# A bilinear form on one core: the first float32 weight group in two transfers, two rows of each partition and then the other six

## The chip, the cores and the metric

The kernel runs on one core of one Trainium2 chip. The metric is the device time of one execution in microseconds, as the median of several runs; smaller is better. The profile's own span, from the first to the last instruction, is a little shorter than that time.

## What is computed

```python
batch, dim_i, dim_j, dim_k = 32, 256, 256, 128
# x: [32, 256], y: [32, 256], weight: [128, 256, 256], all float32
out = np.einsum('bi,bj,kij->bk', x, y, weight)   # [32, 128]
```

The weight is 128 x 256 x 256 x 4 bytes = 33.6 MB and is read once. x, y and the result are small beside it (32, 32 and 16 KB).

## The kernel before

The 128 values of k are laid out as 4 blocks of 32 "groups". A group g is one slice of the weight in SBUF of 128 partitions x 8 rows of 256 values (IC = 8 rows, J = 256), 1 MB in float32, or 8 KB in each partition. For each group TensorE multiplies the 8 rows, one after the other, by a 128 x 128 matrix built from x, and adds them up in PSUM; VectorE multiplies the sum by y and reduces it to one column of the result.

The matmuls take bfloat16. Thirty of the 32 groups come by GpSimd's queue, whose transfers turn float32 into bfloat16 on the way. Two groups, 0 and 16, come as float32 by the queues of SyncE and ScalarE and are then cast by ScalarE. All transfers are placed at the head of the program, ahead of everything else on their engines.

```python
LOADS = (                       # GpSimd's transfers: groups, first row, last row
    ((8, 24), 0, 8),
    ((4, 12, 20, 28), 0, 8),
    (tuple(range(2, 32, 4)), 0, 8),
    (tuple(range(1, 32, 4)), 0, 8),
    ((3, 11, 19, 27), 0, 8),
    ((7, 23), 0, 8),
    ((15,), 0, 8),
    ((31,), 0, 4), ((31,), 4, 6), ((31,), 6, 7), ((31,), 7, 8),
)
FIRST = (0, 16)                 # the two float32 groups
# ... cut ...
    w_sb = sbuf("w_sb", [P, G, IC * J], bf16)
    w_f = sbuf("w_f", [P, len(FIRST), IC * J], f32)
# ... cut ...
    hw = [
        nc.scalar.dma_start(out=x_sb, in_=x).then_inc(s_x, 16).ins,
    ]
    for n, (g, queue) in enumerate(zip(FIRST, (nc.sync, nc.scalar))):
        hw.append(
            queue.dma_start(
                out=w_f[:, n:n + 1, :], in_=rows_of((g,)),
            ).then_inc(s_f[n], 16).ins
        )
# ... cut: hw and GpSimd's transfers are moved to the head of the program ...
    for n, g in enumerate(FIRST):           # ScalarE casts the float32 groups
        for h in range(2):
            lo, hi = h * IC * J // 2, (h + 1) * IC * J // 2
            c = act.copy(out=w_sb[:, place_of[g], lo:hi], in_=w_f[:, n, lo:hi])
            if h == 0:
                c._wait_ge(s_f[n], 16)
            c.then_inc(s_act, 1)
# ... cut: VectorE builds the matrix from x, and y4 from y ...
    pe.wait_ge(s_act, 2 * len(FIRST))
    pe.wait_ge(s_dve, t_x)
    # for each unit of 16, 8, 4, 2, 1 and 1 groups: matmuls over 8 rows, each waiting for
    # its groups' transfer, then VectorE's multiplication by y4 and reduction
# ... cut ...
    sp.dma_start(out=out_v, in_=acc)._wait_ge(s_dve, n_dve).then_inc(s_out, 16)
```

The six units of TensorE are of 16, 8, 4, 2, 1 and 1 groups. The first holds groups 0 and 16 and all that GpSimd's first three weight transfers bring; the last is group 31, which comes in four small pieces.

Of the kernel before, what the change touches and what calls it, by code (L numbers as in the profile page):

```python
# [29 lines left out]
)  # L30

FIRST = (0, 16)
BANKS = 8


@with_exitstack
def kernel(
# [7 lines left out]
    nc = tc.nc  # L45
# [8 lines left out]
    _, J = y.shape  # L54
# [11 lines left out]
    def sbuf(name, shape, dtype):  # L66
        return nc.alloc_sbuf_tensor(name, shape, dtype).ap()

    def rows_of(groups):


        step = G // len(groups)
        assert all(g == groups[0] + n * step for n, g in enumerate(groups))
        v = weight.rearrange("(u s) (ip ic) j -> s ip u (ic j)", s=step, ic=IC)
        return v[groups[0]]

    def w_of(groups):
        at = [place_of[g] for g in groups]
        step = at[1] - at[0] if len(at) > 1 else 1
        assert all(a == at[0] + n * step for n, a in enumerate(at))  # L80
        return w_sb[:, at[0]:at[-1] + 1:step, :]

    w_sb = sbuf("w_sb", [P, G, IC * J], bf16)
    w_f = sbuf("w_f", [P, len(FIRST), IC * J], f32)
    x_sb = sbuf("x_sb", [B, I], f32)
# [10 lines left out]
    acc = sbuf("acc", [P, G], f32)  # L96
    ps = nc.alloc_psum_tensor("ps", [P, BANKS, 2, J], f32).ap()

# [4 lines left out]
        for s, (groups, lo, hi) in zip(s_w, LOADS) for g in groups for ic in range(lo, hi)  # L103
    }
    s_f = [nc.alloc_semaphore(f"f{g}") for g in FIRST]
    s_x = nc.alloc_semaphore("x")
# [14 lines left out]
            out=w_of(groups)[:, :, lo * J:hi * J],  # L121
            in_=rows_of(groups)[:, :, lo * J:hi * J],
# [6 lines left out]
    hw = [  # L129
        nc.scalar.dma_start(out=x_sb, in_=x).then_inc(s_x, 16).ins,  # L130
    ]
    for n, (g, queue) in enumerate(zip(FIRST, (nc.sync, nc.scalar))):
        hw.append(
            queue.dma_start(
                out=w_f[:, n:n + 1, :], in_=rows_of((g,)),
            ).then_inc(s_f[n], 16).ins
        )
    for ins in [*hw, *sw]:
        tc.no_tile_sem_insts.add(ins.name)

# [8 lines left out]
    for blk in blocks:  # L149
# [20 lines left out]
        out=ident, in_=ident, compare_op=mybir.AluOpType.not_equal, fill=1.0,  # L170
# [3 lines left out]

    for n, g in enumerate(FIRST):
        for h in range(2):
            lo, hi = h * IC * J // 2, (h + 1) * IC * J // 2
            c = act.copy(out=w_sb[:, place_of[g], lo:hi], in_=w_f[:, n, lo:hi])  # L178
            if h == 0:
                c._wait_ge(s_f[n], 16)  # L180
            c.then_inc(s_act, 1)


# [2 lines left out]
    def done(ins):  # L186
# [6 lines left out]
        out=x_rep,  # L193
        in_=x_sb.rearrange("b (ip ic) -> b ic ip", ic=IC).unsqueeze(3)
        .to_broadcast([B, IC, IP, KK]),
    )._wait_ge(s_x, 16))
    for q in range(Q):
        c = v.transpose(  # L198
            out=xt[q * 32:(q + 1) * 32, :, :],
            in_=x_rep[:, :, q * IP // Q:(q + 1) * IP // Q, :],  # L200
        )
# [4 lines left out]
        out=mask, in_=ident.rearrange("p (ip kk) -> p kk ip", kk=KK), axis=AX, op=add,  # L206
    )._wait_ge(s_pool, 2))

    for kk in range(KK):
        c = v.tensor_scalar(  # L210
            out=xblk[:, :, :, kk], in0=xt, scalar1=mask[:, kk:kk + 1],
            scalar2=None, op0=mult,
        )
# [6 lines left out]
        out=yt, in_=y_sb.rearrange("b (jb j) -> b jb j", j=32),  # L220
    )._wait_ge(s_y, 16))
    t = done(v.tensor_copy(  # L222
        out=y_rep, in_=yt.unsqueeze(3).to_broadcast([B, J // 32, B, KK]),
    )._wait_ge(s_dve, t))
    BQ = B // Q
    for q in range(Q):
        c = v.transpose(  # L227
            out=y4[q * 32:(q + 1) * 32, :].rearrange("p (jb j) -> p jb j", j=32),
            in_=y_rep[:, :, q * BQ:(q + 1) * BQ, :],
        )  # L230
# [5 lines left out]
    def product(out, lhsT, rhs, first, last, load):  # L236
        return pe.add_instruction(mybir.InstMatmult(  # L237
            name=nc.get_next_instruction_name(), engine=mybir.EngineType.PE,
            ins=[pe.lower_ap(rhs), pe.lower_ap(lhsT)], outs=[pe.lower_ap(out)],
            start_tensor_calc=first, stop_tensor_calc=last,  # L240
            tile_size=(P, P), tile_position=(0, 0), ldweights=load,
        ))

    pe.wait_ge(s_act, 2 * len(FIRST))
    pe.wait_ge(s_dve, t_x)
    at_dve = t_x
    n_pe = 0
    freed = [0] * BANKS
    landed = set()
    p0 = bank = 0  # L250
    held = None
    for u, unit in enumerate(UNITS):

        n_g = len(unit)
        n_b = (n_g + 1) // 2
        if bank + n_b > BANKS:
            bank = 0
# [8 lines left out]
        for n_step, (ic, h) in enumerate(steps):  # L266
            n = n_g // n_b
# [7 lines left out]
            for s in need[:-1]:  # L275
                pe.wait_ge(s, 16)
            c = product(
                ps[:, bank + h, :n, :],
                xblk[:, ic, :, :].rearrange("p b kk -> p (b kk)"),
                w_sb[:, p0 + o:p0 + o + n, ic * J:(ic + 1) * J],  # L280
                first=(ic == order[0]), last=(ic == order[-1]), load=(held != ic),
            )
# [10 lines left out]
        if n_g > 1:  # L293
            t = done(v.tensor_tensor(  # L294
                out=prod, in0=sums, in1=y4.unsqueeze(1).to_broadcast([P, n_g, J]), op=mult,
# [3 lines left out]
                out=acc[:, unit[0]:unit[-1] + 1:unit[1] - unit[0]], in_=prod, axis=AX, op=add,  # L299
            )._wait_ge(s_dve, t))  # L300
        else:
            done(v.tensor_tensor_reduce(  # L302
                out=prod[:, 0, :], in0=sums[:, 0, :], in1=y4, scale=1.0, scalar=0.0,
# [44 lines left out]
```

## Time and profile before

| | before |
|---|---|
| time, median of 3 runs | 84.98 us (84.90 to 85.03) |
| span of the profiled execution | 83.4 us |
| TensorE matmul busy | 32.5 us (39%) |
| VectorE busy | 25.2 us (30%) |
| ScalarE busy | 5.2 us (6%) |
| GpSimd busy | 8.8 us (11%) |
| read from HBM | 33.62 MB |
| GpSimd's queue: packets, share of the 16 DMA engines | 4432, 94.4% |
| SyncE's queue | 288, 3.5% |
| ScalarE's queue | 192, 3.3% |
| float32 group from SyncE, issue to landing | 4.9 us |
| float32 group from ScalarE, issue to landing | 8.3 us |

Busy times are shares of the span; they overlap and don't add up to it. A transfer has two ends in the profile: the instruction with which an engine issues it, and its packets on the 16 DMA engines, which come later. Both are given in microseconds from the first instruction. The GB/s row counts the bytes written, so a transfer that turns float32 into bfloat16 shows half of what it reads. SyncE does nothing between its first transfer and the output.

### The profile page before, as it was taken

How to read it: one execution, taken by the hardware profiler on the slowest of the kernel's cores; microseconds unless marked ns; L12 is line 12 of the kernel's file. 1: busy time of each engine (PE TensorE's matmuls, PEld its weight loads, DVE VectorE, ACT ScalarE, POOL GpSimd, SP SyncE). 2: the span in 40 equal slices, each digit the busy share in tenths (PEclk: the TensorE clock that was granted, in tenths of full speed). 3: DMA queues.
4: the chain of work that ended last, by engine and by line, in shares of the span. 5: the costliest groups of instructions: out<-in, count | busy, mean ns of one | idle time of the engine just before them, and what ended most of it. 6: DMA issues, size and time to landing. Idle time of an engine off the chain costs nothing.

```text
span 83.4 us, 257 instructions
## 1 busy us (share of the span) xinstructions
PE 32.5 (39%) x136; PEld 4.3 (5%) x43; DVE 25.2 (30%) x28; ACT 5.2 (6%) x5; POOL 8.8 (11%) x18
## 2 busy tenths in 40 slices
PE   0000000000000000000099999996029999884780
PEld 0000000000000000000000000000000110112330
DVE  0009450000292000000000000003999800999932
ACT  0019930000000000000000000000000000000000
POOL 5999600000000000000000000000000000000000
PEclk9999999999999999999999999999995799999998
DMA  4999999999999999999999999999999999999980
GB/s 122 393 370 293 214 214 212 216 218 212 218 218 216 212 216 216 212 218 214 212 214 218 210 220 214 214 214 216 212 214 218 212 214 216 212 216 214 197 118 8
DMA packets 4912, 17.91 MB, mean 215 GB/s; under 512 B 384, under 2 KB 800, under 8 KB 4656
## 3 DMA queue, kind: packets, MB, share of 16 engines
q0 software_dynamic: 4432, 15.76, 94.4%
q1 hardware_dynamic: 288, 1.07, 3.5%
q10 hardware_dynamic: 192, 1.08, 3.3%
HBM read 33.62 MB, written 0.02 MB: 403 GB/s over the span
## 4 chain that ended last, share of the span: by engine, by line
DMA 46%; PE 39%; DVE 6%; POOL 3%; another core or an unknown queue 3%; issue 2%; POOLq 0%
DMA w_sb<-in_weight_dram 46%; PE ps L237 39%; DVE tmp L294 5%; POOL w_sb L120 2%; POOL y_sb L127 1%; DVE tmp L302 1%; POOL const-float32-0.0 L332 0%; POOLq L332 0%; POOL const-uint8-127 L332 0%; POOL const-float32-1.0 L332 0%; DVE acc L302 0%
## 5 line engine op out<-in xcount | busy, mean ns | idle before, releaser
L237 PE MATMUL ps<-w_sb,xblk 128*128 128x512 bf16 (+1 forms) x136 | 32.5, 396 | 48.9 <-DMA w_sb<-in_weight_dram 44.2
L294 DVE TENSOR_TENSOR tmp<-ps,y 128x4096 f32<-128x4096 f32 (+3 forms) x4 | 8.6, 2156 | 36.7 <-PE ps L237 36.6
L298 DVE TENSOR_REDUCE acc<-tmp 128x16 f32<-128x4096 f32 (+3 forms) x4 | 8.6, 2154 | 0.1
L237 PEld LDWEIGHTS ps<-w_sb,xblk 128*128 128x128 bf16 x43 | 4.3, 101 | 76.9 <-DMA w_sb<-in_weight_dram 42.7
L120 POOL DMA_DIRECT2D w_sb<-in_weight_dram x11 | 7.6, 707 | 0.6 <-issue 0.6
L178 ACT CAST w_sb<-w_f 128x1024 bf16<-128x1024 f32 x4 | 3.9, 1040 | 0.0
L219 DVE STREAM_TRANSPOSE yt<-y_sb 32x256 f32<-32x256 f32 x1 | 0.4, 433 | 10.9 <-DMA y_sb<-in_y_dram 10.9
L192 DVE COPY x_rep<-x_sb 32x1024 f32<-32x1024 f32 x1 | 0.8, 790 | 6.1 <-PEq L332 6.1
L227 DVE STREAM_TRANSPOSE y<-y_rep 32x256 f32<-32x256 f32 x4 | 1.7, 435 | 0.1
L198 DVE STREAM_TRANSPOSE xt<-x_rep 32x256 f32<-32x256 f32 x4 | 1.7, 435 | 0.1
L178 ACT ACT_TABLE_LOAD x1 | 1.3, 1283 | 6.0 <-PEq L332 6.0
L210 DVE TENSOR_SCALAR xblk<-xt,mask 128x256 bf16<-128x256 f32 x4 | 1.4, 499 | 0.0
L302 DVE CUSTOM_DVE_ANT_0 tmp<-ps,y 128x256 f32<-128x256 f32 x2 | 0.8, 424 | 1.6 <-PE ps L237 1.6
L222 DVE COPY y_rep<-yt 32x1024 f32<-32x1024 f32 x1 | 0.7, 682 | 0.0
L205 DVE TENSOR_REDUCE mask<-ident 128x4 f32<-128x128 f32 x1 | 0.4, 382 | 1.0 <-POOL ident L169 1.0
L127 POOL DMA_DIRECT2D y_sb<-in_y_dram x1 | 0.5, 534 | 0.0
L168 POOL MEMSET ident<- 128x128 f32 x1 | 0.3, 302 | 0.0
L169 POOL TENSOR_SCALAR_AFFINE_SELECT ident<-ident 128x128 f32<-128x128 f32 x1 | 0.3, 287 | 0.1
L302 DVE DVE_READ_ACCUMULATOR2_ANT acc<- 128x1 f32 x2 | 0.2, 84 | 0.0
L332 POOL MEMSET const-float32-0.0<- 128x1 f32 x1 | 0.1, 98 | 0.2 <-issue 0.2
L332 POOL MEMSET const-bfloat16-1.0<- 128x1 bf16 x1 | 0.1, 101 | 0.0
L332 POOL MEMSET const-uint8-127<- 128x1 uint8 x1 | 0.1, 101 | 0.0
(1 smaller groups left out, 0.1 us busy)
## 6 DMA issues: line engine op xcount, KB each, us to landing
w_sb<-in_weight_dram POOLq DMA_DIRECT2D x2, 4096.0 KB, 48.0
w_sb<-in_weight_dram POOLq DMA_DIRECT2D x2, 2048.0 KB, 43.3
w_sb<-in_weight_dram POOLq DMA_DIRECT2D x2, 1024.0 KB, 40.9
w_f<-in_weight_dram SPq DMA_DIRECT2D x1, 1024.0 KB, 4.9
w_f<-in_weight_dram ACTq DMA_DIRECT2D x1, 1024.0 KB, 8.3
w_sb<-in_weight_dram POOLq DMA_DIRECT2D x1, 512.0 KB, 72.1
w_sb<-in_weight_dram POOLq DMA_DIRECT2D x1, 256.0 KB, 72.7
w_sb<-in_weight_dram POOLq DMA_DIRECT2D x1, 128.0 KB, 72.9
```

Source lines behind the costliest of these rows:

```text
L120: nc.gpsimd.dma_start(out=w_of(groups)[:, :, lo * J:hi * J], in_=rows_of(groups)[:, :, lo * J:hi * J],).then_inc(s, 16).ins
L127: sw.insert(2, nc.gpsimd.dma_start(out=y_sb, in_=y).then_inc(s_y, 16).ins)
L178: c = act.copy(out=w_sb[:, place_of[g], lo:hi], in_=w_f[:, n, lo:hi])
L192: t = done(v.tensor_copy(out=x_rep, in_=x_sb.rearrange("b (ip ic) -> b ic ip", ic=IC).unsqueeze(3) .to_broadcast([B, IC, IP, KK]),)._wait_ ...
L198: c = v.transpose(out=xt[q * 32:(q + 1) * 32, :, :], in_=x_rep[:, :, q * IP // Q:(q + 1) * IP // Q, :],)
L210: c = v.tensor_scalar(out=xblk[:, :, :, kk], in0=xt, scalar1=mask[:, kk:kk + 1], scalar2=None, op0=mult,)
L222: t = done(v.tensor_copy(out=y_rep, in_=yt.unsqueeze(3).to_broadcast([B, J // 32, B, KK]),)._wait_ge(s_dve, t))
L227: c = v.transpose(out=y4[q * 32:(q + 1) * 32, :].rearrange("p (jb j) -> p jb j", j=32), in_=y_rep[:, :, q * BQ:(q + 1) * BQ, :],)
L237: return pe.add_instruction(mybir.InstMatmult(name=nc.get_next_instruction_name(), engine=mybir.EngineType.PE, ins=[pe.lower_ap(rhs), pe.l ...
L294: t = done(v.tensor_tensor(out=prod, in0=sums, in1=y4.unsqueeze(1).to_broadcast([P, n_g, J]), op=mult,)._wait_ge(s_pe, n_pe))
L298: done(v.tensor_reduce(out=acc[:, unit[0]:unit[-1] + 1:unit[1] - unit[0]], in_=prod, axis=AX, op=add,)._wait_ge(s_dve, t))
L302: done(v.tensor_tensor_reduce(out=prod[:, 0, :], in0=sums[:, 0, :], in1=y4, scale=1.0, scalar=0.0, op0=mult, op1=add, accum_out=acc[:, uni ...
```

## The change

SyncE's float32 group, one transfer of 8 rows (8 KB) of each partition, is cut into two on the same queue: rows 0 and 1 first, then rows 2 to 7. ScalarE's group stays whole. Both pieces count up the same semaphore, and the first cast of that group waits for 32 in place of 16. The purpose is to get the first bytes of the weight moving sooner: the first transfer that SyncE hands out is a small one.

```diff
 FIRST = (0, 16)
+
+FIRST_ROWS = (((0, 2), (2, 8)), ((0, 8),))
 BANKS = 8
@@
-    for n, (g, queue) in enumerate(zip(FIRST, (nc.sync, nc.scalar))):
-        hw.append(
-            queue.dma_start(
-                out=w_f[:, n:n + 1, :], in_=rows_of((g,)),
-            ).then_inc(s_f[n], 16).ins
-        )
+    for n, pieces in enumerate(FIRST_ROWS):
+        for lo, hi in pieces:
+            hw.append(
+                (nc.sync, nc.scalar)[n].dma_start(
+                    out=w_f[:, n:n + 1, lo * J:hi * J],
+                    in_=rows_of(FIRST[n:n + 1])[:, :, lo * J:hi * J],
+                ).then_inc(s_f[n], 16).ins
+            )
@@
-                c._wait_ge(s_f[n], 16)
+                c._wait_ge(s_f[n], 16 * len(FIRST_ROWS[n]))
```

Everything else, the instructions of TensorE, VectorE, ScalarE and GpSimd among it, is as before; SyncE has one issue more.

## The prediction

> **What bounds the kernel now.** I read the chain of waits first, then the waits, then the first microseconds cut into short stretches. In the chain of work that ended last, in order of time (start us, length us, what), these pieces carry the end:
>
> ```profile
> 3.18 38.65 DMA w_sb<-in_weight_dram
> ...
> 74.77 1.28 another core or an unknown queue
> ...
> 77.98 0.49 another core or an unknown queue
> ...
> 79.55 0.17 another core or an unknown queue
> ...
> 81.44 0.42 DVE tmp L302
> ```
>
> TensorE works in bursts and between them waits for something that is not an engine. The timeline names it: before the matmuls at 76.09, 78.51 and 79.76 us the releaser is the transfer of w_sb, with idle times of 1.32, 0.53 and 0.22 us. So the end hangs on the last bytes of the weight. The page's row of the 16 DMA engines' busy share over 40 slices of 2.1 us, and the rate below it, say whether that stream ever rests:
>
> ```profile
> DMA  4999999999999999999999999999999999999980
> GB/s 122 393 370 293 214 214 212 216 218 212 218 218 216 212 216 216 212 218 214 212 214 218 210 220 214 214 214 216 212 214 218 212 214 216 212 216 214 197 118 8
> ```
>
> It rests in the first slice and after the weight is in, nowhere else. The rate halves after the fourth slice because GpSimd's transfers read float32 and write bfloat16, and the row counts bytes written: 214 written are about 428 read. The end is therefore: when the stream gets going, plus the bytes over a fixed rate, plus a tail. The change touches only the first term and, a little, the second. The start, from the timeline (start us, length us of the issuing instruction):
>
> ```profile
> 0.00 0.63 SPq L134 DMA_DIRECT2D w_f<-in_weight_dram  x1
> 0.12 0.42 ACTq L130 DMA_DIRECT2D x_sb<-in_x_dram  x1
> ...
> 0.58 0.56 ACTq L134 DMA_DIRECT2D w_f<-in_weight_dram  x1
> 1.05 1.60 POOL L120 DMA_DIRECT2D w_sb<-in_weight_dram  x2 [0.61 <-issue]
> ```
>
> and the same time in stretches of 0.2 us; the last two columns are the DMA share and GB/s:
>
> ```profile
> 1.00:1.20 0.20, 0.00 (x0) 0.00 (x0) 0.00 (x0) 0.00 (x0) 0.15 (x1) 1.00 0.08 31
> 1.20:1.40 0.20, 0.00 (x0) 0.00 (x0) 0.00 (x0) 0.00 (x0) 0.20 (x1) 1.00 0.43 128
> 1.40:1.60 0.20, 0.00 (x0) 0.00 (x0) 0.00 (x0) 0.00 (x0) 0.20 (x1) 1.00 2.02 492
> 1.60:1.80 0.20, 0.00 (x0) 0.00 (x0) 0.00 (x0) 0.00 (x0) 0.20 (x1) 1.00 0.50 123
> 1.80:2.00 0.20, 0.00 (x0) 0.00 (x0) 0.00 (x0) 0.00 (x0) 0.20 (x2) 1.00 0.66 210
> 2.00:2.20 0.20, 0.00 (x0) 0.00 (x0) 0.00 (x0) 0.00 (x0) 0.20 (x1) 1.00 1.01 410
> ```
>
> A packet is counted where it starts, so single values jump. The sum from 1.0 to 2.0 us is (31 + 128 + 492 + 123 + 210) x 0.2 us = 197 KB; at the 410 GB/s that the next twelve stretches have on average (their sum is 4919), that is 0.48 us of work. The stream behaves as if it had begun at full rate at 2.00 - 0.48 = 1.52 us after the first instruction. That 1.52 us is all the change can win from. The packet records of the trace say what is in it: x, 32 packets of 1 KB, starts at 1.16 us, 1.04 us after its issue began; the first 8 KB packet of the SyncE transfer starts at 1.42 us, 1.42 us after its issue began. The first packets of this transfer take up to 594 ns, later ones mostly 309 to 345. ScalarE's float32 group starts only at 4.19 us, when SyncE's is nearly through, and GpSimd's first packet comes at 5.48 us.
>
> **What the Trainium skill says.** "DMA: Bandwidth & Descriptors", section "Latency and other measured facts", puts the first byte of a transfer from SyncE or ScalarE at about 0.6 us. The trace has 1.04 us (x) and 1.42 us (weight) from the beginning of the issuing instruction, and 0.63 and 0.79 us from its end; only the second count is near it. The same page, section "Issuing engines are not separate DMA queues", says that all issuers share the same 16 DMA engines and that more issues save only sequencer time. The trace agrees: once going, the rate is about 410 GB/s whoever issued. Its section "Rules for kernel authors" advises one large transfer rather than several small ones, which speaks against the change. Its section "Why a DMA increments its semaphore by 16 and not by 1" warns that of two transfers sharing a semaphore only the full count says that all has landed; the changed kernel does wait for 32, the full count, so no half-landed group is read.
>
> **The change part by part.** It removes one SyncE issue of 128 rows of 8 KB and puts two in its place: 128 rows of 2 KB, then 128 rows of 6 KB. Bytes, matmuls, casts and the other queues stay.
>
> Gained: an earlier first packet. The weight issue took 0.63 us and its first packet came 0.79 us later. The output transfer, also 128 rows from SyncE but of 128 B each, took 0.35 us to issue at 81.90 us and had its first packet at 82.74 us, 0.84 us after the issue began. So 128 rows need not cost 1.42 us; the longer rows, or being first, do. If the issue grows with the bytes of a row, a row of 2 KB lies a quarter of the way: 0.35 + (0.63 - 0.35)/4 = 0.42 us. First packet 0.63 to 0.79 us later, thus at 1.05 to 1.21 us instead of 1.42: a gain of 0.21 to 0.37 us, middle 0.29.
>
> Does a hole follow? The first piece is 8 packets of 2 KB per DMA engine. At 313 ns for 8 KB (the median in this queue) that is 8 x 78 = 0.63 us, plus some 0.28 us by which the first packet exceeds a later one (594 - 313): it lasts till about 1.13 + 0.63 + 0.28 = 2.04 us. The second issue can begin at 0.42 us and, taken like the whole one, has its first packet 1.42 us later, at 1.84 us, before the first piece ends. ScalarE's group is issued at 0.58 us as well. No hole is expected.
>
> Paid: packets. Each DMA engine has 8 more data packets and one more completion. The x packets of 1 KB took 44 ns where 313/8 = 39 would be in proportion, so 5 ns of overhead each; GpSimd's packets that write 1 KB from 2 KB took 98 ns where 324/4 = 81 is in proportion, 17 ns. So 9 more packets cost 9 x 5 = 0.05 to 9 x 17 = 0.15 us per engine, middle 0.10 us, and this lies on the path because the stream never rests.
>
> Beside the path: the extra issue on SyncE (some 0.5 us), which has nothing to do until 81.90 us; and w_f landing later. It landed 4.9 us after issue; should ScalarE's group now go in between, it might land at about 8.2 us. The four casts (1.04 us each, from 7.33 us) would then end about 1 us later, at 12.2 us, and TensorE doesn't start until 41.87 us.
>
> Sum: -0.29 + 0.10 = -0.19 us. I round it up a little in favour of the change, as the late first packets may shorten too, and take -0.23: 84.98 - 0.23 = 84.75 us.
>
> **The rivals.** First, the first packet doesn't come sooner: 1.42 us is set by being the first issue, or by x, whose packets run at 1.16 to 1.39 us on most engines just ahead. Against it stands that ScalarE's second issue, not its first, took 0.56 us for the long rows, and its first, with 32 short ones, 0.42. For it: the output transfer differs from the weight's in being late and alone as well as in row length, so the trace holds no clean pair; also one DMA engine had both its x packet and its first weight packet only at 1.93 us, which is no matter of row length. Then only the packets' cost remains: 84.98 + 0.10 = 85.08 us.
>
> Second, a hole between the pieces: the second issue waits behind x and ScalarE's issue, and its first packets pay the start again, up to 0.28 us (594 - 313). With the gain of 0.29 and the cost of 0.10 this makes 85.07 us. Against it: ScalarE's group would fill the hole, because it is queued from 1.14 us on.
>
> Third, a hidden gain: the stream ends earlier but TensorE doesn't follow. TensorE idles 1.32 us for the transfer at 76.09 us and 0.30 us at 71.16 us, so a stream earlier by 0.2 or 0.3 us pulls every later start. I give this little weight; it would leave 84.98 us.
>
> Fourth, a large loss, if 6 KB rows ran badly. The group is a 32nd of the weight, some 2.5 us of the stream. It would have to run at under 60% of its rate to cost 2%: 2.5/0.6 = 4.2 us. Nothing in the trace points there.
>
> **Range and chances.** The main line gives from -0.37 + 0.05 = -0.32 to -0.21 + 0.15 = -0.06 us, the rivals 0 to +0.15 us. I give the main line three chances in five. With the spread of the runs before (84.90 to 85.03) the range is 84.45 to 85.12 us. A change of 2% is 1.7 us, more than the whole 1.52 us before the stream starts, so faster by over 2% is practically shut out, and slower by over 2% needs the fourth rival: 0.01 faster, 0.98 within 2%, 0.01 slower.
>
> **What would show each step right or wrong.** Right: in the changed profile SyncE shows two issues, the first shorter than 0.63 us; short stretches show weight traffic before 1.4 us and no dip between 1.8 and 2.4 us; the effective start worked out as above falls from 1.52 to about 1.25 us; and the matmuls' waits for w_sb near the end, and the last w_sb packet at 80.79 us, come some 0.2 us earlier. The first issue as long as before, or a first packet at 1.4 us, proves the first rival; a dip after 2 us the second; an earlier last packet with the same end the third. The prediction is wrong if the time rises clearly although the first packet comes earlier: then the packets cost more than 17 ns each, or the order of the queues matters in a way that this profile doesn't show.

## Result and profile after

| | before | after |
|---|---|---|
| time, median | 84.91 us (84.69 to 85.03, 6 runs) | 87.21 us (87.06 to 102.13, 6 runs) |
| ratio after / before, 95% interval | | 1.0272 (1.0253 to 1.0292) |
| span of the profiled execution | 83.4 us | 85.9 us |
| last weight packet ends | 80.79 us | 83.28 us |
| SyncE's float32 group, first packet to last packet's end | 1.42 to 4.57 us | 1.40 to 4.99 us (2 KB rows), 5.43 to 12.20 us (6 KB rows) |

Ratios leave out executions over 1.5% above the fastest of their kernel: here the one of 102.13 us (granted clock 0.76), below two of flat_64_64 and one of pitch_10k.

The change costs 2.3 us. Two rows of the page show where: the busy share of the DMA engines and GB/s in 40 slices of 2.15 us, changed kernel.

```profile
DMA  2699999999999999999999999999999999999930
GB/s 61 189 354 320 293 226 214 216 216 218 216 214 216 218 214 218 214 218 214 214 214 214 214 216 214 214 214 214 214 216 214 216 214 214 218 210 213 193 47 8
```

The first two slices move 61 and 189 GB/s; before, they moved 122 and 393. From the seventh slice on the rate is that of before. So the loss is made in the first microseconds, up to about 5 us, and never given back. Cut finer, DMA share and GB/s in the last two columns, first the changed kernel:

```profile
1.40:2.00 0.60, 0.00 (x0) 0.00 (x0) 0.00 (x0) 0.00 (x0) 0.60 (x2) 1.00 0.42 126
2.00:3.00 1.00, 0.00 (x0) 0.00 (x0) 0.00 (x0) 0.00 (x0) 1.00 (x2) 1.00 0.37 96
3.00:4.00 1.00, 0.00 (x0) 0.00 (x0) 0.00 (x0) 0.00 (x0) 1.00 (x2) 1.00 0.90 254
4.00:5.00 1.00, 0.00 (x0) 0.00 (x0) 0.00 (x0) 0.00 (x0) 1.00 (x3) 1.00 0.85 281
5.00:6.00 1.00, 0.00 (x0) 0.00 (x0) 0.00 (x0) 0.00 (x0) 1.00 (x2) 1.00 1.03 424
```

and three of the same stretches before:

```profile
1.40:2.00 0.60, 0.00 (x0) 0.00 (x0) 0.00 (x0) 0.00 (x0) 0.60 (x2) 1.00 1.06 275
2.00:3.00 1.00, 0.00 (x0) 0.00 (x0) 0.00 (x0) 0.00 (x0) 1.00 (x2) 1.00 1.04 426
3.00:4.00 1.00, 0.00 (x0) 0.00 (x0) 0.00 (x0) 0.00 (x0) 1.00 (x2) 1.00 0.99 401
```

From 2 to 3 us, when all data packets are 2 KB rows, the changed kernel moves 96 GB/s where 426 were moved. The engines are then busy for 0.37 of the time, and 59% of the 2 KB packets took no more than 84 ns, about a quarter of the 309 ns of most 8 KB packets: much of the time is lost between the packets. The transfer's 16 completion packets of 4 bytes, which fit one for each DMA engine, show when each share of the 2 KB rows was done: eight at 2.72 to 3.31 us, the other eight at 3.87 to 4.99 us. ScalarE's group, from 3.12 us on, doesn't reach full rate before 5 us. Summed over the packet records, a packet's bytes spread evenly over its time, 1.75 MB had been read by 6.0 us before and 1.08 MB after; the missing 0.67 MB are 1.6 us at the 430 GB/s that were read from 10 to 75 us.

The profiled end came 2.5 us later; the remaining 0.9 us of that is unevenness. A transfer counts as complete with the last of 16 counts on its semaphore, one from each DMA engine: in the changed kernel the 16th count of the transfer that TensorE first waits for came at 44.32 us, and TensorE started at 44.37 us. The times of the first and the last of these 16 counts, from the trace's semaphore events:

```
transfer                         before              after
GpSimd's first weight transfer   11.97 to 12.45 us   13.14 to 14.95 us
GpSimd's last weight transfer    80.59 to 81.07 us   81.75 to 83.56 us
```

The earliest count is 1.2 us late, the latest 2.5 us, the mean of the 16 1.6 us, and all three stay so through 70 us. That fits engines that each keep a fixed share of every transfer; the records don't name the engines, so this is not shown. The end waits for the latest count. The chain that ended last shows the shift passing through (start us, length us, what; changed kernel):

```profile
3.17 41.15 DMA w_sb<-in_weight_dram
...
77.31 1.20 another core or an unknown queue
...
80.44 0.53 another core or an unknown queue
...
82.04 0.18 another core or an unknown queue
...
83.93 0.42 DVE tmp L306
```

The first wait for the weight grew by 2.50 us (from 38.65), the last VectorE step starts 2.49 us later (from 81.44), and the three waits in between that stand here are within 0.08 us of those before.

The timeline of the issues (changed kernel) answers the first question of the prediction:

```profile
0.00 1.27 SPq L137 DMA_DIRECT2D w_f<-in_weight_dram  x2
0.12 0.41 ACTq L132 DMA_DIRECT2D x_sb<-in_x_dram  x1
...
0.58 0.60 ACTq L137 DMA_DIRECT2D w_f<-in_weight_dram  x1
...
12.83 3.88 ACT L182 CAST w_sb<-w_f 128x1024 bf16<-128x1024 f32 x4 [5.51 <-DMA w_f<-in_weight_dram]
```

SyncE's two issues take 0.63 and 0.59 us (1.27 us with the pause between them); the small one is no shorter than the whole one was. The casts wait for the 6 KB rows and end at 16.7 us, far from TensorE's start at 44.37 us.

### The profile page after: what moved, and what is told of

The parts are those of the page before. It is cut to its first block, busy times and chain, and to the rows that moved or that the text cites. A ratio compares the mean times of both kernels' runs of the same rounds, so it can differ in the third digit from the quotient of the medians.

```text
span 85.9 us, 258 instructions
## 1 busy us (share of the span) xinstructions
PE 32.0 (37%) x136; PEld 4.2 (5%) x43; DVE 25.1 (29%) x28; ACT 5.2 (6%) x5; POOL 8.8 (10%) x18
## 3 DMA queue, kind: packets, MB, share of 16 engines
q10 hardware_dynamic: 192, 1.08, 3.4%
## 4 chain that ended last, share of the span: by engine, by line
DMA 48%; PE 37%; DVE 6%; another core or an unknown queue 3%; POOL 3%; issue 1%; POOLq 0%
DMA w_sb<-in_weight_dram 48%; PE ps L241 37%; DVE tmp L298 5%; POOL w_sb L122 2%; POOL y_sb L129 1%; DVE tmp L306 0%; POOL const-float32-0.0 L336 0%; POOLq L336 0%; POOL const-uint8-127 L336 0%; POOL const-float32-1.0 L336 0%; DVE acc L306 0%
## 5 line engine op out<-in xcount | busy, mean ns | idle before, releaser
L241 PE MATMUL ps<-w_sb,xblk 128*128 128x512 bf16 (+1 forms) x136 | 32.0, 392 | 51.9 <-DMA w_sb<-in_weight_dram 47.2
```

Of the source, the lines that this page charges most:

```text
L241: return pe.add_instruction(mybir.InstMatmult(name=nc.get_next_instruction_name(), engine=mybir.EngineType.PE, ins=[pe.lower_ap(rhs), pe.l ...
```

## Experiments

All change only SyncE's and ScalarE's float32 groups or x. "Loss" is the ratio's excess over 1, with its interval, in us at 84.9 us. "First packet" is the start of the first packet of SyncE's group. Where the text says that other values are read, the columns of group 0 come out different from what the kernel should compute; the number of bytes is the same.

**parts_64_64.** Two transfers, but cut by partitions.

```diff
-out=w_f[:, n:n + 1, :], in_=rows_of((g,))
+out=w_f[lo:hi, n:n + 1, :], in_=rows_of((g,))[lo // KK:hi // KK]   # (0, 64), (64, 128)
```

> SyncE's float32 group in two transfers as well, but cut by partitions (64 and 64), so that every packet keeps its 8 KB and there are 128 of them as before. Theory of the packet rate (SyncE's and ScalarE's transfers hand out packets at some 47 a microsecond whatever their size, so that 2 KB packets starve the DMA engines): 84.9 us, as before, within 0.4. Theory of the second transfer (the cost is the second issue and the handover from one transfer to the next): 87.2 us, as in the changed kernel.

86.11 us, ratio 1.0142 (1.0119 to 1.0165): loss 1.0 to 1.4 us, so neither theory. The packets say why it is no clean test: with the engines busy all the time on average from 2 to 6 us, an 8 KB packet of SyncE's took 439 ns on average where 350 was the mean before. Writing 64 of the 128 partitions brings in something of its own (see flat_64_64).

**one_2k.** One transfer, packets of 2 KB.

```diff
-out=w_f[:, n:n + 1, :], in_=rows_of((g,))
+out=w_g[:, :, :2 * J], in_=flat       # w_g: 4 pieces of 512 values, 16 values between them; flat: 1 MB of k = 0..3
```

> One transfer on SyncE as before, but its 1 MB lands in pieces set 64 bytes apart, so that it takes 512 packets of 2 KB; to keep the access pattern within three dimensions it reads 1 MB that lies together (k = 0 to 3) in place of the rows of group 0, so the columns of group 0 hold other values. Theory of the packet rate: 512 packets at 47 a microsecond are 10.9 us at about 100 GB/s; until GpSimd's packets come at about 5.5 to 6.2 us some three quarters of 4 to 5 us are lost: 88 to 88.6 us. Theory of the second transfer: one issue, so 84.9 us, plus at most 0.4 us for 24 more packets on each DMA engine.

84.96 us, ratio 1.0009 (1.0002 to 1.0015). The queue's line on the page and two stretches show 512 small packets, which reach full rate from 3 us on:

```profile
q1 hardware_dynamic: 672, 1.07, 3.8%
```

```profile
2.00:3.00 1.00, 0.00 (x0) 0.00 (x0) 0.00 (x0) 0.00 (x0) 1.00 (x2) 1.00 0.80 285
3.00:4.00 1.00, 0.00 (x0) 0.00 (x0) 0.00 (x0) 0.00 (x0) 1.00 (x2) 1.00 1.04 403
```

403 GB/s in 2 KB packets is 197 packets a microsecond. The theory of the packet rate, which I had formed from the changed kernel's 47 a microsecond, is out. What remained of it was a limit on rows in place of packets, since each row of a partition holds four packets here.

**rows_4_4 and rows_6_2.** Other cuts.

```diff
-FIRST_ROWS = (((0, 2), (2, 8)), ((0, 8),))
+FIRST_ROWS = (((0, 4), (4, 8)), ((0, 8),))     # rows_6_2: (0, 6), (6, 8)
```

> The cut at row 4 in place of row 2: 128 packets of 4 KB first, then 128 of 4 KB. Theory of the packet rate: the first piece takes 2.7 us as with 2 KB packets but moves 0.52 MB in it, 1.28 us of work at 410 GB/s, so 1.4 us are lost in place of 2.1: 86.3 us. Theory of the second transfer: 87.2 us.

> The same two pieces in the other order of size: six rows (6 KB packets) first, two rows (2 KB packets) second. Theory of the packet rate: the first piece moves 0.79 MB in 2.7 us, 1.92 us of work, 0.8 us lost; the 2 KB packets come when GpSimd's packets are there to fill in: 85.7 us. Theory of the second transfer: 87.2 us.

86.12 us, 1.0155 (1.0132 to 1.0178), and 85.57 us, 1.0088 (1.0063 to 1.0113). The loss falls with the size of the first piece: 2.3, 1.3, 0.7 us for 2, 4, 6 rows. From 2 to 3 us, rows_4_4:

```profile
2.00:3.00 1.00, 0.00 (x0) 0.00 (x0) 0.00 (x0) 0.00 (x0) 1.00 (x2) 1.00 1.03 238
```

rows_6_2:

```profile
2.00:3.00 1.00, 0.00 (x0) 0.00 (x0) 0.00 (x0) 0.00 (x0) 1.00 (x2) 1.00 0.99 301
```

96, 238, 301 and 426 GB/s for 2, 4, 6 and 8 KB out of every 8 KB: about in proportion to the share taken. With half rows the engines count as busy all the time and still move 238. In this run that speaks for slow reads and not for starved engines, while in the changed kernel the engines were busy for only 0.37 of the same stretch; the records don't say what they waited for there. The price of a second transfer as such would have been the same in all three. Both times are within 0.2 us of what the theory of the packet rate forecast (86.3 and 85.7 us), though one_2k had put that theory out. That is luck: the first pieces of 2, 4 and 6 KB rows did end at about the same time (4.99, 4.62 and 4.46 us), but not by a packet rate.

**flat_2_6.** The pieces of the changed kernel from unbroken stretches.

```diff
-in_=rows_of(FIRST[n:n + 1])[:, :, lo * J:hi * J]
+in_=flat(lo, hi)          # 256 KB, then 768 KB without gaps, from k = 0..3
```

> The changed kernel's two pieces (2 KB and 6 KB rows on SyncE), but each read from one unbroken stretch of the weight (256 KB and 768 KB, k = 0 to 3) in place of the first 2 KB of every 8 KB, so the columns of group 0 hold other values. Theory of addresses (2 KB out of every 8 KB fall on few of the memory's channels, and the reads are slow): no loss, 84.9 to 85.2 us. Theory of rows (the rows of a transfer from SyncE or ScalarE are handed out one by one, some 48 a microsecond, whatever they hold, so that 2 KB rows starve the DMA engines): as the changed kernel, 87.2 us.

84.64 us, 0.9974 (0.9963 to 0.9986): the whole loss is gone, with two transfers and 128 packets of 2 KB, which now take from 1.00 to 2.41 us. The theory of rows is out. But the source also lost a dimension of its pattern, the issues became shorter (0.83 us for both), and the 6 KB rows came ahead of ScalarE's group, from 2.16 us on, so more than the addresses had changed. Against the kernel before, this run is even 0.1 to 0.3 us faster, which is about what the prediction expected of the cut.

**act_2_6.** The same cut on ScalarE's group.

```diff
-FIRST_ROWS = (((0, 2), (2, 8)), ((0, 8),))
+FIRST_ROWS = (((0, 8),), ((0, 2), (2, 8)))
```

> The cut in the other float32 group: SyncE's stays whole, ScalarE's comes in rows 0 to 1 and 2 to 7. The 2 KB packets then come from about 4.2 us on, GpSimd's from about 5.5 us. Theory of rows: 128 rows take 2.7 us, and in the 1.3 us until GpSimd's packets come three quarters are lost: 1.0 us, 85.9 us. Theory of the start (starving belongs to the first microseconds of the program, in which every transfer runs up slowly): 84.9 to 85.2 us. Theory of the second transfer (any cut costs by its handover): 85.6 us or more.

86.37 us, 1.0176 (1.0161 to 1.0192). The start is no part of it. Of the three theories only that of the second transfer had room for so much, and flat_2_6 had two transfers without the loss. Here the small rows come while the engines run at full rate, which makes it the clearest picture of their cost:

```profile
4.80:6.00 1.20, 0.00 (x0) 0.00 (x0) 0.00 (x0) 0.00 (x0) 1.20 (x3) 1.00 1.01 106
2.40:4.00 1.60, 0.00 (x0) 0.00 (x0) 0.00 (x0) 0.00 (x0) 1.60 (x3) 1.00 1.01 399
```

All engines are busy in both stretches; with 8 KB rows they move 399 GB/s, with 2 KB of every 8 KB 106. A 2 KB packet took 278 ns on average.

**rows_2_2_4.** Three pieces.

```diff
+FIRST_ROWS = (((0, 2), (2, 4), (4, 8)), ((0, 8),))
```

> SyncE's group in three pieces, 2, 2 and 4 rows. If SyncE's and ScalarE's transfers take turns, the order is 2 KB, ScalarE's 8 KB, 2 KB, 4 KB, and up to GpSimd's first packets all is as in the changed kernel. Theory of rows: 87.2 us, within 0.3; if SyncE's second piece goes ahead of ScalarE's group, 88.3 us. Theory of the second transfer: another 0.7 to 2.3 us for another handover, 87.9 to 89.5 us.

87.34 us, 1.0286 (1.0269 to 1.0304): a third transfer adds almost nothing to the changed kernel's 87.21. It is the time that the theory of rows forecast, which flat_2_6 puts out all the same. The later pieces run beside GpSimd's packets, which would fill what they leave: the engines stayed busy for 0.98 to 1.08 of each microsecond from 6 to 11 us.

**x_last.** x behind ScalarE's group, in the kernel before.

```diff
-hw = [nc.scalar.dma_start(out=x_sb, in_=x).then_inc(s_x, 16).ins]
+# the same line behind the loop over the float32 groups
```

> The kernel before, with x issued behind ScalarE's float32 group in place of ahead of it. Theory of rows: x's 32 rows no longer go ahead of the weight's, the first weight packet comes at 1.16 to 1.25 us in place of 1.42 us, and the end moves with it: 84.7 us. Rival (the first weight packet is as late as its own issue makes it): first packet at 1.42 us, 84.9 us.

84.93 us, 1.0012 (1.0003 to 1.0021), first weight packet at 1.405 us. x does not hold the weight back; the rival is right.

**strided_2_6.** The region and the two dimensions of flat_2_6, with the gaps back.

```diff
+in_=v.rearrange("(p c) -> p c", p=P)[:, lo * J:hi * J]     # v: 1 MB of k = 0..3
```

> As flat_2_6, from the same unbroken 1 MB, but cut as in the changed kernel: the first piece takes the first 2 KB of every 8 KB, the second the other 6 KB, so two dimensions of the pattern as in flat_2_6 but addresses with gaps (the columns of group 0 hold other values). Theory of addresses (2 KB out of every 8 KB are read at a quarter of the rate): 86.5 to 87.2 us. Theory of the pattern (three dimensions in the pattern of the source make the rows slow to hand out, two do not): 84.6 us as flat_2_6.

85.26 us, 1.0058 (1.0043 to 1.0073). Between the two: the gaps cost something (the 2 KB rows take from 1.00 to 3.19 us instead of 2.41), but 0.5 us and not 2.3. One difference stood out: the shorter issues put SyncE's 6 KB rows ahead of ScalarE's group, from 1.88 us on. sp_order, below, has that order with the four k of group 0, 8 MB apart, and loses 0.8 us, so where the rows lie may count beside their pitch; no run separates this.

**packed_2_6.** The four k of group 0, three dimensions, no gaps.

```diff
+v = weight.rearrange("(u s) i j -> s u (i j)", s=G)[0]
+in_=v[:, IP * lo * J:IP * hi * J].rearrange("u (ip c) -> ip u c", ip=IP)
```

> All bytes of group 0 are read, in 2 KB and 6 KB packets and with three dimensions as in the changed kernel, but the first piece takes the first 64 KB of each of the four k of the group without gaps and the second the other 192 KB, so rows land in other partitions and the columns of group 0 hold other values. Theory of addresses: 84.6 to 85.1 us. Theory of the pattern: 87.2 us.

85.10 us, 1.0038 (1.0025 to 1.0051). Same packets, dimensions, issue times (1.26 us for both) and order of the transfers as in the changed kernel, and 2.0 of its 2.3 us are gone (loss 0.2 to 0.4 us). Only the addresses differ:

```profile
1.40:2.00 0.60, 0.00 (x0) 0.00 (x0) 0.00 (x0) 0.00 (x0) 0.60 (x2) 1.00 0.64 148
2.00:3.00 1.00, 0.00 (x0) 0.00 (x0) 0.00 (x0) 0.00 (x0) 1.00 (x2) 1.00 1.10 399
```

399 GB/s in the stretch where the changed kernel moves 96. The theory of the pattern is out.

**flat_64_64 and flat_whole.** Unbroken source for the cut by partitions, and for the single transfer.

```diff
+in_=flat[lo:hi]     # flat_64_64, (0, 64) and (64, 128);  flat_whole: in_=flat
```

> parts_64_64 again (two transfers of 64 partitions, 8 KB rows), with SyncE's group read from one unbroken 1 MB (k = 0 to 3; the columns of group 0 hold other values). If parts_64_64 lost its time to addresses (half of each of four stretches 8 MB apart), it is gone: 84.7 to 85.1 us. If it lost it on the side of SBUF (16 DMA engines write into half of the partitions): 86.1 us as parts_64_64.

> One transfer for SyncE's group as in the kernel before, read from the unbroken 1 MB as in flat_2_6 (the columns of group 0 hold other values). Tells whether the first packet at 1.0 us and the 0.1 us of flat_2_6 come from the pattern of the source or from the small first piece. From the pattern: first packet at about 1.0 to 1.1 us and 84.6 us. From the small piece: first packet at 1.4 us and 84.8 us.

flat_64_64: 87.41 us, its four runs from 86.40 to 87.88 us, ratio 1.0235 (1.0192 to 1.0278), from two of them. Unbroken addresses don't cure the cut by partitions. That leaves the side of SBUF, which no run here shows by itself. flat_whole: 84.65 us, 0.9991 (0.9978 to 1.0003), and its issue is short (timeline):

```profile
0.00 0.39 SPq L135 DMA_DIRECT2D w_f<-in_weight_dram  x1
```

Its first packet comes at 1.01 us, with a whole 8 KB row. So the bytes of a row don't set the length of the issue and the first packet. Nor do gaps: strided_2_6, with gaps, issued its 2 KB rows in 0.38 us (first packet at 1.00 us), one_2k, without, took 0.65 us (1.44 us). What goes with the short issues is a pattern of two dimensions, but flat_64_64 had two as well and took 0.55 us for its first issue, so this is not settled. And a first packet 0.4 us sooner brought no measurable gain. The first 14 packets took 0.69 to 1.16 us each (309 ns was the median), little was begun behind them,

```profile
1.40:2.00 0.60, 0.00 (x0) 0.00 (x0) 0.00 (x0) 0.00 (x0) 0.60 (x2) 1.00 0.18 68
```

and by 6 us 1.74 MB had been read, as before.

**pitch_10k and pitch_16k.** Is it gaps as such?

```diff
+wide = weight.rearrange("(u s) i j -> u (s i j)", s=G)[:, :IP * 2560]      # pitch_16k: 4096
+wide = wide.rearrange("u (ip c) -> ip u c", ip=IP)[:, :, :2 * J]           # first piece only
```

> The changed kernel, but the first piece takes 2 KB out of every 10 KB instead of every 8 KB, over the same four k and with the same pattern of three dimensions; the second piece is as in the changed kernel (two rows of group 0 hold other values). Theory of spread (what counts is how evenly the addresses of one piece fall: starts a multiple of 8 KB apart reach only a share of the memory, starts 10 KB apart reach all of it): as packed_2_6, 85.0 to 85.4 us. Theory of gaps (any gap between one 2 KB read and the next costs): 87.2 us as the changed kernel.

> As pitch_10k, but 2 KB out of every 16 KB. Theory of spread: half the share that 2 KB of every 8 KB reach, so the 128 reads take up to twice as long and more is lost before GpSimd's packets come: 88 to 89.5 us. Theory of gaps: 87.2 us.

85.34 us, 1.0054 (1.0033 to 1.0076), and 87.07 us, 1.0257 (1.0241 to 1.0272). From 2 to 3 us, pitch_10k:

```profile
2.00:3.00 1.00, 0.00 (x0) 0.00 (x0) 0.00 (x0) 0.00 (x0) 1.00 (x2) 1.00 1.17 432
```

pitch_16k:

```profile
2.00:3.00 1.00, 0.00 (x0) 0.00 (x0) 0.00 (x0) 0.00 (x0) 1.00 (x2) 1.00 0.67 123
```

Gaps as such aren't it: 2 KB of every 10 KB are read at 432 GB/s, 2 KB of every 8 or 16 KB at 96 and 123. The pitch, the distance from one start to the next, makes the difference. But the dose went wrong for the theory of spread: it expected 16 KB to be worse than 8 KB, 88 us or more, and it is about the same.

**sp_order.** All on SyncE, the 6 KB rows directly behind the 2 KB rows.

```diff
-(nc.sync, nc.scalar)[n].dma_start(
+nc.sync.dma_start(
```

> The changed kernel's pieces and addresses, but all on SyncE in the order rows 0 to 1, rows 2 to 7, then the other float32 group, so that the 6 KB pieces follow right behind the 2 KB pieces in place of behind the other group. If the order has a part in the loss (the rest of each 8 KB, which would fill the idle share, is held back behind ScalarE's group): 85.3 to 85.8 us. If the slow first piece alone makes the loss: 87.2 us.

85.73 us, 1.0098 (1.0081 to 1.0115): of 2.3 us, 0.8 are left, with the changed kernel's pieces and addresses (ScalarE's group now stands in SyncE's queue, behind them). The 6 KB rows start at 2.75 us in place of 5.43:

```profile
2.00:3.00 1.00, 0.00 (x0) 0.00 (x0) 0.00 (x0) 0.00 (x0) 1.00 (x2) 1.00 0.68 172
3.00:4.00 1.00, 0.00 (x0) 0.00 (x0) 0.00 (x0) 0.00 (x0) 1.00 (x2) 1.00 0.97 348
```

The first piece is as slow until 2.7 us and ends at 2.74 to 4.10 us on the 16 engines, but what follows recovers sooner, and the counts lie closer together (last minus first of the 16 counts of GpSimd's first transfer: 1.05 us, against 1.81).

## Why the prediction was wrong

**The step that failed** is the length of the first piece: "At 313 ns for 8 KB (the median in this queue) that is 8 x 78 = 0.63 us". It carried the rate of 8 KB rows over to 2 KB rows, which is only right if a row is a row wherever it lies. The forecast end of the piece was 2.04 us; it ended at 2.72 to 3.31 us on eight engines and at 3.87 to 4.99 us on the other eight. In packed_2_6, same packets without the 8 KB pitch, it took from 1.40 to 2.87 us, nearer to the step. The cause shown is the pitch of 8 KB between the starts (packed_2_6 and pitch_10k cure it, pitch_16k doesn't). That such starts meet in a part of the memory only is argued, not shown, and the equal loss at 16 KB speaks against its simplest form. The Trainium skill, "DMA: Bandwidth & Descriptors", section "Latency and other measured facts", tells of low rates, in copies between HBM tensors with rows of 16 KiB, at row pitches that are large powers of two, from 2 MiB on, and that 4 KiB of padding restores the rate; it calls its own explanation an inference. The runs here show the like at 8 and 16 KB for reads of 2 KB (96 and 123 GB/s, against 432 at 10 KB). The prediction drew on that section for the first byte only.

**No hole** failed with it: the dip forecast as the sign of the second rival came, but inside the first piece (DMA share 0.37 from 2 to 3 us). The second rival had the hole between the pieces, from a start to be paid again and worth 0.28 us, and set against it that ScalarE's group would fill it. ScalarE's group did come next, from 3.12 us, but unevenly, and it pushed the 6 KB rows, which would have filled the gap, back to 5.43 us. sp_order, where they followed directly, is 1.5 us faster than the changed kernel.

**The earlier first packet** failed as well: 1.40 us in place of the 1.05 to 1.21 forecast, since the issue stayed at 0.63 us. The first rival was right there, though not for its reason: x_last clears x, and flat_whole has the first issue at 0.39 us with 8 KB rows, so being first isn't it, nor the row's length. How much an earlier first packet is worth stays unclear: nothing measurable in flat_whole, 0.1 to 0.3 us in flat_2_6, which differs in more.

**The packets' cost** agrees with its low end: one_2k has 24 more data packets on each engine and loses 0.02 to 0.13 us, 1 to 5 ns each, though its source is another one than before.

**Beside the path** held, though w_f was there for the casts only at 12.8 us and not at about 8.2: the casts still ended at 16.7 us, before TensorE's start at 44.37. **The third rival** was rightly given little: TensorE followed the stream, to 0.01 us.

**The fourth rival** put a large loss at 0.01 because the 6 KB rows would need less than 60% of the rate. It looked at the wrong piece: the 2 KB rows ran at 96/426 = 23%.

**The range** doesn't follow from its own terms: from -0.32 to +0.15 us, with the spread of the runs, is 84.58 to 85.18 us, not 84.45 to 85.12.

What stays open: what makes these pitches slow, why 16 KB is no worse than 8 KB, why half of the engines are so much later in the changed kernel, why the loss shows as idle engines there and as long packets in act_2_6, and the last 0.3 us of packed_2_6.

## What to carry to other kernels

A transfer's speed can depend on where its rows start, not only on their size and number: before cutting a load along its rows, look at the pitch that each piece is left with, and cut so that a piece stays unbroken in memory. If such a piece is needed, issue the piece that fills its gaps directly behind it; here that saved 1.5 of 2.3 us. On a kernel that waits for its stream to the end, what is lost in the first microseconds comes back at the end, at the pace of the DMA engine that fell behind most.

## What the hardware showed that was not expected

Reading 2 KB of every 8 KB ran at 106 GB/s with all 16 engines busy, 2 KB of every 10 KB at 432. The issue of a 1 MB transfer took 0.63 us with the source of the kernel before and 0.39 us with one unbroken stretch in a pattern of two dimensions. The spread of the 16 counts of one transfer, 1.81 us at 13 to 15 us, was again 1.81 us at 82 to 84 us.
